# A diffusion block's front: first rows and gate weights loaded amid the input, sums that begin at the bias, more work on ACT, the weight transform ahead of its use

## The chip, the core and the metric

The kernel runs on one core of one Trainium2 chip. TensorE (PE) multiplies, VectorE (DVE), ScalarE (ACT) and GpSimd (POOL) work element by element, SyncE (SP) issues most DMAs. The metric is the device time of one execution in microseconds; the median of several runs counts.

## The reference

One layer: a normalised and modulated input goes through one projection into a Fourier group and a windowed attention group, both gated, and through one output projection. `x` is 1024 x 1024, `ctx` 256 x 1024, all fp32.

```python
def _ada(cond, w_ada, b_ada):
    mod = jax.nn.silu(cond) @ w_ada + b_ada
    return jnp.split(mod, 3, axis=-1)

sh_x, sc_x, g_x = [t[:, None, :] for t in _ada(c, w_ada[l], b_ada[l])]
sh_c, sc_c, g_c = _ada(c_ctx, w_ada[l], b_ada[l])
xn = _rms_norm(x, norm_g[l]) * (1.0 + sc_x) + sh_x
cn = _rms_norm(ctx, norm_g[l]) * (1.0 + sc_c) + sh_c
fx_in, fx_gate, qx, kx, vx, nx_gate = _split_proj(xn @ w_in[l])
fc_in, fc_gate, qc, kc, vc, nc_gate = _split_proj(cn @ w_in[l])
...
f_out = _fourier(fx_in, w_four[l]) * jax.nn.silu(fx_gate)
na_out = _neighbourhood_attention(qx, kx, vx, kc, vc, rel_bias[l]) * jax.nn.silu(nx_gate)
x_new = x + g_x * (jnp.concatenate([f_out, na_out], axis=-1) @ w_out[l])
```

`_fourier` is the real part of a 2-D DFT over positions and the 128 channels of each of 4 groups, then `@ w_four`.

## The kernel before

Every fp32 operand of a matmul is split into a rounded high part and the low rest (names ending in `h` and `l`: `xnh`, `xnl`, `wh`, `wl`), and a product is three matmuls: high by high, high by low, low by high. ACT mostly makes the high part (a cast or copy), DVE or POOL the low one (a subtraction).

The program runs in stages.

- *Input and turning.* `load_x` loads 8 tiles of `x` (128 rows each), `normalise` squares and sums them (ACT `Square`, or a DVE dot of `x` with itself), takes the root on POOL and scales the tile; `turn_x` transposes it on TensorE, and the results are copied to `xrt` (8 column blocks of 128, over all rows). `cond_row` broadcasts the 1 x 1024 row `c` over the partitions by a K=1 matmul, with the silu on ACT, into `sbc`.
- *ada dots.* For each of the 8 column blocks `i`, `load_wd` loads two 128 x 1024 tiles of the transposed `w_ada` (shift and scale), and `ada` issues a DVE dot of each with `sbc` (for `x`) and with `scc` (for the context), and behind each pair the three column operations of `ada_out`. A 256 KB gate weight comes with each block (`load_gate`, its cast and subtraction in `cut`).
- *Gate products* (L365). `modulate(i)` makes `xnh` (ACT), the modulated `xrt` (ACT or DVE) and `xnl` (DVE) in two halves of the rows, and 24 matmuls per block add to 8 PSUM banks.
- *Folds.* The DFT over positions is folded: `fold_zero`, `fold_ends`, `fold_middle` add and subtract rows of `xrt` (DVE); `fold_weights` transforms the Fourier columns of the weight by matmuls (`pw`, L469) and splits the result (`wab_h`, `wab_l`); `fold_products` multiplies (`pe`, `po`, `p`). `fourier_gate` takes silu of the gate products on ACT (L462).
- `turn_columns` finishes the transform over columns (`pp`, `pq`), with `w4h`/`w4l`, the transformed `w_four` (made from `wf` tiles by an add and a subtract on POOL, L595 and L597), ready for `ga` and `gb`.
- *Projections* of q, k, v and gates, the context's keys and values (`context_input`, `context_block`), and from some 160 us on the attention of 8 heads, interleaved with the rest of the projections and `gate_dot`, and last the output product.

The order on each engine is written by a planner that runs when the program is built: `chain` gives a list of steps with an engine and an assumed time, `when` and `at` hold a step until marks are set or a time is reached, and `issue` picks, whenever an engine is free by the planner's clock, the ready step with the lowest rank. Where a step may run on either of two engines (a list in the `chain`), whichever is free first takes it. The assumed times and ranks (`TC`, `RX`, `RG`, `RM`, `XS`, ... at the top) thus decide the order; on the chip each engine then runs its instructions in that fixed order and waits on semaphores. `XS` says how many tiles of `x` are loaded ahead of the first weights. SP issues loads in program order.

Of the kernel before, what the change touches and what calls it, by code (L numbers as in the profile page):

```python
# [11 lines left out]
F32 = mybir.dt.float32  # L12
# [7 lines left out]
P = 128  # L20
DM = 1024
KT = 8
TC, RX, RG, RM = 3.0, 2, 0, 2
TW, RT0, RT1, RT2, RH, D0, D1, NC = 4, 0, 4, -1, 1, 0, 0, 0
N0 = (3, 3, 2, 2)
XS = (8,)
LAG, PW, EB = 1, 8, 2
NP, NM, TL, WL = (0, 0, 0, 1, 0, 0, 0, 1), (6,) * 8, 0, 3
P0 = 1
# [15 lines left out]
def tile_hybrid_block(  # L45
# [47 lines left out]
    pool.memset(mhalf, -0.5)  # L93
    gsc = const.tile([P, 1], F32, name="gsc")
# [187 lines left out]
    def far_dot(wd, s, col, key, rank):  # L282

        chain((DVE_, 1.14, lambda: dot(wd, s, junk, col)), mark(*key), rank=rank)

    def ada(i, s, dsh, dav, name, rank):
        cols = wa.tile([P, 2], F32, name=f"cols{name}{i}")
        for j in range(2):
            when(((name, "s"), ("wd", i, j) if name == "x" else ("x", i, j)), lambda j=j: far_dot(wds[i, j], s, cols[:, j:j + 1], (name, i, j), rank))
        when(((name, i, 0), (name, i, 1), "vec"), lambda: chain((DVE_, 0.27, lambda: ada_out(i, cols, dsh, dav)), mark(name, i), rank=rank))  # L290

    def cond_row():

        for hf in range(2):
            hs = slice(hf * 512, hf * 512 + 512)
            pt = bank("pc", hf)
            mm(pt, ones1, sbc[0:1, hs], start=True, stop=True)
            chain((ACT_, 0.48, lambda hs=hs, pt=pt: act.activation(sbc[:, hs], pt, AF.Silu)), mark("x", "s") if hf else (lambda: None), rank=0)
# [14 lines left out]
    def load_gate(i):  # L313
# [3 lines left out]
        def cut():  # L317
            gate_w[i] = wh, wl = halves()
            chain(copy_by(512, WHO["gc"], wh, wr), mark("wh", i),
                  (DVE_, 0.6, lambda: dve.tensor_tensor(out=wl, in0=wr, in1=f(wh), op=ALU.subtract)),  # L320
# [3 lines left out]
    def turn_x(t):  # L324
        for hf in range(2):
            pt = bank("pt", hf if t < 4 else 1)
            for i in range(4):
# [4 lines left out]
                [(DVE_, 0.6, lambda: dve.tensor_copy(o, v)), (ACT_, 0.48, lambda: act.copy(o, v))],  # L332
                mark("turned", t, hf), rank=RT0 * t + (RT1 if hf else 0) + (RT2 if t > 3 else 0)))

    def normalise(t):
        x = xs[t]
        ss = wa.tile([P, 2], F32, tag="ss", bufs=8, name="ss")
        rs = wa.tile([P, 1], F32, tag="rs", bufs=8, name="rs")
        chain([(ACT_, 1.04, lambda: act.activation(sqx, x, AF.Square, accum_out=ss[:, 0:1])), (DVE_, 1.14, lambda: dot(x, x, junk, ss[:, 0:1]))],
              (DVE_, 0.07, lambda: dve.tensor_scalar(out=ss[:, 1:2], in0=ss[:, 0:1], scalar1=1.0 / DM, scalar2=EPS, op0=ALU.mult, op1=ALU.add)),  # L340
              (POOL_, 0.46, lambda: pool.tensor_tensor(out=rs, in0=ss[:, 1:2], in1=mhalf[:, 0:1], op=ALU.pow)),
              (DVE_, 0.67, lambda: dve.tensor_scalar_mul(x, x, rs)),
              (PE_, 1.7 if t < TW else 0.9, lambda: turn_x(t)), rank=RT0 * t + (RT2 if t > 3 else 0))

    def modulate(i):
# [6 lines left out]
        for hf in range(2):  # L352
# [1402 lines left out]
```

## Time and profile before

| | |
|---|---|
| runs | 605.64 us median of 3 (604.29 to 609.53) |
| profiled execution | 601.05 us, of which its span 599.3 |
| mean granted clock of TensorE | 0.98 |
| busy, share of the span | PE 91%, DVE 79%, ACT 59%, POOL 37% |
| instructions | PE 2923, DVE 967, ACT 742, POOL 196 |
| HBM read, written | 59.35 MB, 8.91 MB |

Times are microseconds from the start of the span. An operation is named by its line, engine, and the tiles it writes and reads (`out<-in`). "Idle before" is how long the engine stood still ahead of an instruction, with the instruction that released it. The busy share is an average over stages with different limits, so the rows below go by stretch. The clock column is the granted clock of TensorE, 1.00 being 2.4 GHz and 0.5 being 1.2 GHz.

### The profile page before, as it was taken

How to read it: one execution, taken by the hardware profiler on the slowest of the kernel's cores; microseconds unless marked ns; L12 is line 12 of the kernel's file. 1: busy time of each engine (PE TensorE's matmuls, PEld its weight loads, DVE VectorE, ACT ScalarE, POOL GpSimd, SP SyncE). 2: the span in 40 equal slices, each digit the busy share in tenths (PEclk: the TensorE clock that was granted, in tenths of full speed). 3: DMA queues.
4: the chain of work that ended last, by engine and by line, in shares of the span. 5: the costliest groups of instructions: out<-in, count | busy, mean ns of one | idle time of the engine just before them, and what ended most of it. 6: DMA issues, size and time to landing. Idle time of an engine off the chain costs nothing. (4 is left out here: it accounts for less than half of the span.)

```text
span 599.3 us, 8648 instructions
## 1 busy us (share of the span) xinstructions
PE 545.4 (91%) x2923; PEld 477.6 (80%) x2923; DVE 471.6 (79%) x967; ACT 353.4 (59%) x742; POOL 222.1 (37%) x196
## 2 busy tenths in 40 slices
PE   6699648899899999979999999999999798999997
PEld 4578538889677988979889889799898586787886
DVE  4999999985899678687895878977779959778342
ACT  6676035364634577767877878868767747654100
POOL 3100004014744635452545533444444937424300
PEclk9999968999999999999999999999999799999999
DMA  8970424025694242112032030321104563213152
GB/s 337 406 281 2 164 82 141 1 84 171 200 306 155 101 123 59 39 33 79 22 102 85 22 89 1 111 66 41 61 2 148 177 224 118 66 55 120 38 194 88
DMA packets 42889, 68.83 MB, mean 115 GB/s; under 512 B 3542, under 2 KB 25430, under 8 KB 42844
## 3 DMA queue, kind: packets, MB, share of 16 engines
q1 hardware_dynamic: 41836, 64.60, 32.1%
q0 software_dynamic: 1008, 3.67, 1.8%
q8 instruction: 23, 0.38, 0.3%
q14 instruction: 22, 0.18, 0.1%
HBM read 59.35 MB, written 8.91 MB: 114 GB/s over the span
## 5 line engine op out<-in xcount | busy, mean ns | idle before, releaser
L797 PE MATMUL pqkv<-wh,xnh 128*128 128x384 f32 x256 | 86.8, 339 | 0.0
L797 PE MATMUL pqkv<-wl,xnh 128*128 128x384 f32 x256 | 86.7, 339 | 0.0
L797 PE MATMUL pqkv<-wh,xnl 128*128 128x384 f32 x256 | 86.1, 336 | 0.0
L1174 ACT ACTIVATE pr<-pr,tr 128x640 f32<-128x640 f32 (+1 forms) x64 | 51.2, 801 | 28.4 <-DVE tr L1170 28.1
L1170 DVE CUSTOM_DVE_ANT_0 pr<-s,bias 128x640 f32<-128x640 f32 (+1 forms) x64 | 50.4, 788 | 21.9 <-PE s L1165 14.5
L703 POOL TENSOR_TENSOR hrs<-hss,mhalf 128x4 f32<-128x4 f32 (+1 forms) x34 | 37.7, 1113 | 60.7 <-DVE hss L700 53.1
L202 DVE TENSOR_TENSOR el<-e,eh 128x384 fp32r<-128x384 f32 (+2 forms) x71 | 50.7, 720 | 11.0 <-ACT eh L207 9.9
L207 ACT CAST eh<-e 128x384 fp32r<-128x384 f32 (+2 forms) x96 | 49.5, 528 | 1.4
L797 PEld LDWEIGHTS pqkv<-wl,xnh 128*128 128x128 f32 x256 | 48.1, 188 | 1.3
L797 PEld LDWEIGHTS pqkv<-wh,xnh 128*128 128x128 f32 x256 | 48.1, 188 | 1.3
L1266 ACT ACTIVATE e<-e 128x384 f32<-128x384 f32 (+1 forms) x64 | 31.5, 496 | 29.1 <-DVE e L1256 28.6
L797 PEld LDWEIGHTS pqkv<-wh,xnl 128*128 128x128 f32 x256 | 48.1, 188 | 0.7
L202 POOL TENSOR_TENSOR el<-e,eh 128x512 fp32r<-128x512 f32 x25 | 32.6, 1306 | 41.1 <-ACT eh L207 41.0
L202 POOL TENSOR_TENSOR wl<-wr,wh 128x384 fp32r<-128x384 f32 (+1 forms) x24 | 30.3, 1265 | 46.4 <-ACT wh L207 28.2
L1256 DVE TENSOR_TENSOR e<-st,biast 128x256 f32<-128x256 f32 (+2 forms) x80 | 34.0, 445 | 7.6 <-PE st L1248 6.8
L1163 PE MATMUL s<-ks,qs 128*128 128x256 f32 (+1 forms) x128 | 30.4, 318 | 9.1 <-DVE tr L1170 8.3
L1163 PEld LDWEIGHTS s<-ks,qs 128*128 128x128 f32 x128 | 23.1, 192 | 16.9 <-DVE tr L1170 13.2
L1247 PE MATMUL st<-qs,ks 128*128 128x512 f32 (+2 forms) x96 | 33.7, 353 | 0.3
L365 PE MATMUL pg<-xnh,w 128*128 128x512 f32 x128 | 31.3, 397 | 2.6 <-ACT xnh L356 2.6
L1248 PE MATMUL st<-qs,ks 128*128 128x512 f32 (+2 forms) x96 | 33.3, 347 | 0.0
L1443 PE MATMUL po<-oh,mh 128*128 128x512 f32 x88 | 32.3, 404 | 0.3 <-DVE gate L825 0.3
L365 PEld LDWEIGHTS pg<-xnh,w 128*128 128x128 f32 x128 | 23.9, 188 | 8.9 <-ACT xnh L356 3.3
(290 smaller groups left out, 1596.8 us busy)
## 6 DMA issues: line engine op xcount, KB each, us to landing
wd<-in_w_ada_t_dram SPq DMA_DIRECT2D x16, 512.0 KB, 8.9
wr<-in_w_in_dram SPq DMA_DIRECT2D x40, 192.0 KB, 2.7
wr<-in_w_in_dram SPq DMA_DIRECT2D x24, 256.0 KB, 4.1
x<-in_xb_dram SPq DMA_DIRECT2D x8, 512.0 KB, 6.4
wdg<-in_w_ada_t_dram SPq DMA_DIRECT2D x8, 512.0 KB, 5.3
owr<-in_w_out_dram SPq DMA_DIRECT2D x16, 256.0 KB, 2.9
y<-in_xb_dram SPq DMA_DIRECT2D x8, 512.0 KB, 6.6
out_dram<-y SPq DMA_DIRECT2D x15, 256.0 KB, 2.1
```

The lines of the kernel that those rows point to most:

```text
L202: return [(e, time(n), lambda eng=eng: eng.tensor_tensor(out=out, in0=in0, in1=in1, op=op)) for e, eng, time in (both[k] for k in who)]
L207: return [(e, time(n), lambda cp=cp: cp(out, in_)) for e, cp, time in (both[k] for k in who)]
L365: mm(pg[j][hf], gate_w[i][w][:, j * P:(j + 1) * P], x[i][:, hs], start=(i == 0 and g == 0), stop=(i == KT - 1 and g == 2))
L703: lambda: pool.tensor_tensor(out=rs[:, 0:nh], in0=ss[:, 0:nh], in1=mhalf[:, 0:nh], op=ALU.pow),
L797: mm(o, x[k][:, ts_], w, start=(k == 0 and n == 0), stop=(k == KT - 1 and n == 2))
L1163: mm(o, qs1[h][:, ts_], ks1[h][:, kk], start=st, stop=sp)
L1170: dve.tensor_tensor_reduce(out=pr, in0=sv, in1=bt, scale=-1.0, scalar=3.0e38, op0=ALU.add, op1=ALU.min, accum_out=tr[:, t:t + 1])
L1174: (ACT_, a_t(nl + CTX) + 0.15, lambda: act.activation(pr, pr, AF.Exp, bias=tr[:, t:t + 1], scale=-1.0, accum_out=sm[:, t:t + 1])),
L1247: mm(s, ks1[h][:, kk], qs1[h][:, qq], start=True, stop=False)
L1248: mm(s, ks2[h][:, kk], qs2[h][:, qq], start=False, stop=True)
L1256: dve.tensor_tensor(out=ew[:, u:v], in0=s3[:, u:v], in1=mixes[p, h][0][:, blocks], op=ALU.add)
L1443: mm(o, mf[k][m][:, ts_], wf[hf][k][w_], start=(k == 0 and n == 0), stop=(k == 3 and n == 2))
```

## The change

- Tiles 0 to 3 of `x` are loaded, then the shift and scale weights and the gate weight of block 0, then tiles 4 to 7 (`XS` is `(4, 8)`). The context's row `c_ctx` is loaded as one row beside `c` and broadcast by `cond_row` on TensorE, in place of a broadcast DMA of 512 KB.
- A dot starts from its bias column (and takes the norm's gain as its scale), so `ada_out` is gone; `vec_in` forms the combined bias once. The normalisation's epsilon is added by an ACT step behind `Square`, or is the start of the dot, in place of a DVE step. `gate_dot` starts from its bias too.
- The scaling of `x` and the copies from PSUM may go to ACT or DVE; the context's modulation is done by two ACT activations in place of a DVE step and an ACT copy. Assumed times of steps are changed.
- The fold stage issues the four gates first, then the eight `fold_weights`, with `fold_zero` and `fold_ends` after the fourth.
- The add and subtract on `wf` move from POOL in the fold stage to DVE in `turn_columns`, behind the splits of `pe` and `po`, and the `w4h`, `w4l` split with them.
- The planner also runs `issue` again for POOL and DVE when they become free after the set-up of the heads.

```diff
-TC, RX, RG, RM = 3.0, 2, 0, 2
...
-XS = (8,)
-LAG, PW, EB = 1, 8, 2
...
+TC, RX, RG, RM = 2.0, 2, 0, 2
...
+XS = (4, 8)
+LAG, EB, TL = 1, 2, 0
+NW = (0, 0, 0, 0, 1, 1, 1, 1)
...
-    def ada_out(i, cols, dsh, dav):
-        k = slice(i, i + 1)
-        dve.tensor_tensor(out=dsh[:, k], in0=cols[:, 0:1], in1=vec[:, V_BSH + i:V_BSH + i + 1], op=ALU.add)
-        dve.tensor_scalar(out=cols[:, 1:2], in0=cols[:, 1:2], scalar1=vec[:, V_BSC + i:V_BSC + i + 1], scalar2=1.0, op0=ALU.add, op1=ALU.add)
-        dve.tensor_tensor(out=dav[:, k], in0=cols[:, 1:2], in1=vec[:, V_NG + i:V_NG + i + 1], op=ALU.mult)
...
+    def dot(wd, s, jk, col, scale=1.0, first=0.0):
+        dve.tensor_tensor_reduce(out=jk, in0=wd, in1=s, scale=scale, scalar=first, op0=ALU.mult, op1=ALU.add, accum_out=col)
...
+    def squares(jk, x, ss):
+
+        act.activation(jk, x, AF.Square, scale=DM ** -0.5, accum_out=ss)
+        act.activation(ss, ss, AF.Identity, bias=epsc)
...
+    def vec_in():
+
+        dve.scalar_tensor_tensor(out=vec[:, V_BSC:V_BSC + KT], in0=vec[:, V_BSC:V_BSC + KT], scalar=1.0, in1=vec[:, V_NG:V_NG + KT], op0=ALU.add, op1=ALU.mult)
...
+        def column(j):
+            if j:
+                dot(wds[i, j], s, junk, dav[:, k], vec[:, V_NG + i:V_NG + i + 1], vec[:, V_BSC + i:V_BSC + i + 1])
+            else:
+                dot(wds[i, j], s, junk, dsh[:, k], 1.0, vec[:, V_BSH + i:V_BSH + i + 1])
...
-        chain([(ACT_, 1.04, lambda: act.activation(sqx, x, AF.Square, accum_out=ss[:, 0:1])), (DVE_, 1.14, lambda: dot(x, x, junk, ss[:, 0:1]))],
-              (DVE_, 0.07, lambda: dve.tensor_scalar(out=ss[:, 1:2], in0=ss[:, 0:1], scalar1=1.0 / DM, scalar2=EPS, op0=ALU.mult, op1=ALU.add)),
-              (POOL_, 0.46, lambda: pool.tensor_tensor(out=rs, in0=ss[:, 1:2], in1=mhalf[:, 0:1], op=ALU.pow)),
-              (DVE_, 0.67, lambda: dve.tensor_scalar_mul(x, x, rs)),
+        chain([(ACT_, 1.44, lambda: squares(sqx, x, ss)), (DVE_, 1.24, lambda: dot(x, x, junk, ss, 1.0 / DM, EPS))],
+              (POOL_, 0.46, lambda: root(rs, ss)),
+              [(ACT_, 1.06, lambda: act.mul(x, x, rs)), (DVE_, 0.75, lambda: dve.tensor_scalar_mul(x, x, rs))],
...
-                [(DVE_, 0.41, lambda: dve.tensor_scalar(out=v, in0=v, scalar1=av[:, k], scalar2=sh[:, k], op0=ALU.mult, op1=ALU.add)),
-                 (ACT_, 0.71, lambda: act.activation(v, v, AF.Identity, scale=av[:, k], bias=sh[:, k]))],
...
+                [(ACT_, 0.81, lambda: act.activation(v, v, AF.Identity, scale=av[:, k], bias=sh[:, k])),
+                 (DVE_, 0.55, lambda: dve.tensor_scalar(out=v, in0=v, scalar1=av[:, k], scalar2=sh[:, k], op0=ALU.mult, op1=ALU.add))],
...
-                dma(scc, c_ctx.broadcast_to([P, DM]))
...
-        fold_zero()
-        for i in range(EB):
-            fold_ends(i)
-        mid = fold_middle()
         for j in range(4):
             fourier_gate(j)
-            for _ in range(N0[j]):
+        mid = fold_middle()
+        for n in range(8):
+            fold_weights(n // 4, n % 4)
+            if n == 3:
+                fold_nyquist(0)
+                fold_zero()
+                for i in range(EB):
+                    fold_ends(i)
+            for _ in range(NW[n]):
                 next(mid)
...
-            if i == WL:
-                pool.tensor_tensor(out=wfr[0], in0=wfr[0], in1=wfr[1], op=ALU.add)
-            if i == WL + 1:
-                pool.tensor_tensor(out=wfr[2], in0=wfr[2], in1=wfr[1], op=ALU.subtract)
...
+        dve.tensor_tensor(out=wfr[0], in0=wfr[0], in1=wfr[1], op=ALU.add)
+        act.copy(w4h[0], wfr[0])
+        dve.tensor_tensor(out=wfr[2], in0=wfr[2], in1=wfr[1], op=ALU.subtract)
+        act.copy(w4h[1], wfr[2])
+        for m in range(2):
+            dve.tensor_tensor(out=w4l[m], in0=wfr[2 * m], in1=f(w4h[m]), op=ALU.subtract)
...
+        for e in (POOL_, DVE_):
+            at(free[e], lambda e=e: issue(e))
...
-        chain((DVE_, 0.33, lambda: dve.tensor_scalar(out=crt[:, i], in0=crt[:, i], scalar1=avc[:, k], scalar2=shc[:, k], op0=ALU.mult, op1=ALU.add)),
-              (ACT_, a_t(256), lambda: act.copy(h, crt[:, i])),
+        chain((ACT_, 0.42, lambda: act.activation(h, crt[:, i], AF.Identity, scale=avc[:, k], bias=shc[:, k])),
+              (ACT_, 0.42, lambda: act.activation(crt[:, i], crt[:, i], AF.Identity, scale=avc[:, k], bias=shc[:, k])),
```

The changed times and the new lists give the engines another order. On ACT, in the gate stage, before (casts of a gate weight are `w_N<-wr_M`, weight 5 the first here and weight 6 the second; `xnh4` is the modulated block 4):

```order
L207 CAST w_509<-wr_400 128x512
L356 ACTIVATE xnh4_338<-xrt1_98,sh_77,av_78 128x16x4x8 x2
L358 ACTIVATE xrt1_98<-xrt1_98,sh_77,av_78 128x16x32 x2
L207 CAST w_547<-wr_417 128x512
L356 ACTIVATE xnh5_339<-xrt1_98,sh_77,av_78 128x16x4x8 x2
```

The same place on ACT now (lines are those of the changed kernel):

```order
L207 CAST w_483<-wr_380 128x512
L207 CAST w_516<-wr_407 128x512
L358 ACTIVATE xnh4_359<-xrt1_100,sh_79,av_80 128x16x4x8 x2
L359 ACTIVATE xrt1_100<-xrt1_100,sh_79,av_80 128x16x32
L358 ACTIVATE xnh5_360<-xrt1_100,sh_79,av_80 128x16x4x8 x2
```

Both casts now stand ahead of block 4, where before the cast of weight 6 stood behind it; the second modulation of one half has gone to DVE.

On ACT, at the end of the gate products, before (`ef` is a fold of the ends, `gate_f` a gate, `h4` the high part of a fold):

```order
L490 CAST x0h_82<-x0_748 128x8
L501 ACTIVATE ef_760<-xrt0_97 128x1
L501 ACTIVATE ef_764<-xrt0_97 128x1
L462 ACTIVATE gate_f_768<-pg00_294 128x512
L462 ACTIVATE gate_f_768<-pg01_353 128x512
L523 CAST h4_771<-s2_773 128x512
```

And now:

```order
L359 ACTIVATE xrt1_100<-xrt1_100,sh_79,av_80 128x16x32
L463 ACTIVATE gate_f_697<-pg00_296 128x512
L463 ACTIVATE gate_f_697<-pg01_374 128x512
L463 ACTIVATE gate_f_700<-pg10_297 128x512
L463 ACTIVATE gate_f_700<-pg11_375 128x512
```

The gates now follow the last modulation at once, and the fold of the ends comes after them.

On DVE, in `turn_columns`, now (before, the two `w4l` rows stood ahead of `al`, and the two `wf` rows were POOL's):

```order
L114 TENSOR_TENSOR bl_1151<-po1_795,bh_1150 128x512
L624 TENSOR_TENSOR wf_671<-wf_671,wf_673 128x1024
L626 TENSOR_TENSOR wf_675<-wf_675,wf_673 128x1024
L629 TENSOR_TENSOR w4l0_1136<-wf_671,w4h0_1134 128x1024
L629 TENSOR_TENSOR w4l1_1137<-wf_675,w4h1_1135 128x1024
L631 CAST w64_1138<-w64_1138 4x512
L632 TENSOR_TENSOR w64_1138<-wfn_693,w64_1138 4x512
```

Four 128 x 1024 operations now stand between `bl` and `w64`.

## Rows read from the trace of the kernel before

**Rows 1.** Busy time by stretch: length; PE, PEld, DVE, ACT, POOL busy (instructions); clock; DMA share; GB/s.

```profile
0.00:24.00 24.00, 13.84 (x68) 9.57 (x68) 15.06 (x34) 16.43 (x30) 7.66 (x16) 1.00 0.94 363
24.00:70.00 46.00, 45.15 (x192) 35.92 (x192) 44.80 (x103) 24.38 (x36) 0.00 (x0) 1.00 0.45 169
70.00:83.00 13.00, 2.58 (x12) 2.50 (x12) 12.69 (x35) 1.27 (x4) 0.00 (x0) 0.64 0.38 128
...
101.00:124.00 23.00, 21.38 (x158) 20.07 (x158) 22.47 (x48) 9.15 (x18) 1.28 (x4) 0.93 0.01 2
...
136.00:160.00 24.00, 21.98 (x140) 20.20 (x140) 16.55 (x32) 13.31 (x30) 15.46 (x12) 1.00 0.65 209
160.00:548.00 388.00, 369.39 (x1971) 328.41 (x1970) 312.36 (x646) 268.79 (x582) 183.22 (x154) 0.99 0.29 92
```

**Rows 2.** What TensorE waited for, whole program: us in total, times, longest.

```profile
PE pw L469 <- ACT gate_f L462: 13.7, 2, 10.4
PE s L1163 <- DVE tr L1170: 8.3, 8, 3.5
```

**Rows 3.** What ACT waited for, 60 to 100 us, same columns.

```profile
ACT ef L501 <- DVE colsc L255: 17.2, 1, 17.2
```

**Rows 4.** Timeline of DVE: start, us, operation, out<-in, form; gate stage.

```profile
28.74 0.68 DVE L320 TENSOR_TENSOR w<-wr,w 128x512 fp32r<-128x512 f32 x1
29.34 0.15 DVE L250 TENSOR_TENSOR sh<-colsx,vec 128x1 f32<-128x1 f32 x1
...
29.73 1.22 DVE L255 CUSTOM_DVE_ANT_0 junk<-wd,sbc 128x1024 f32<-128x1024 f32 x1
30.87 0.09 DVE L255 DVE_READ_ACCUMULATOR2_ANT colsx<- 128x1 f32 x1
30.87 0.55 DVE L357 TENSOR_SCALAR xrt<-xrt,av,sh 128x512 f32<-128x512 f32 x1
```

**Rows 5.** Timeline of POOL, 95 to 100.2 us.

```profile
95.46 2.42 POOL L595 TENSOR_TENSOR wf<-wf 128x1024 f32<-128x1024 f32 x1
97.84 2.34 POOL L597 TENSOR_TENSOR wf<-wf 128x1024 f32<-128x1024 f32 x1
```

**Rows 6.** Timeline of DVE, the fold stage.

```profile
82.80 0.69 DVE L499 TENSOR_TENSOR ef<-xrt 128x512 f32<-128x512 f32 x1
...
86.90 0.69 DVE L526 TENSOR_TENSOR l<-s,h 128x512 fp32r<-128x512 f32 x1
...
97.13 3.60 DVE L526 TENSOR_TENSOR l<-s,h 128x512 fp32r<-128x512 f32 x1
```

**Rows 7.** Timeline of TensorE in the front; in brackets, idle before and releaser.

```profile
24.07 1.20 PE L365 MATMUL pg<-xnh,w 128*128 128x512 f32 x4 [1.82 <-ACT xnh L356]
...
80.50 3.67 PE L469 MATMUL pw<-cst,wtr 128*128 128x128 f32 x16 [10.42 <-ACT gate_f L462]
87.41 7.20 PE L469 MATMUL pw<-cst,wtr 128*128 128x128 f32 x48 [3.25 <-ACT gate_f L462]
...
100.79 0.45 PE L546 MATMUL pe<-wab_h,l 128*128 128x260 f32 x1 [2.54 <-DVE l L526]
```

**Rows 8.** Busy time by stretch, columns as in rows 1, at low clock.

```profile
100.90:104.50 3.60, 3.60 (x17) 3.52 (x18) 3.56 (x8) 1.07 (x2) 0.00 (x0) 0.53 0.03 7
472.90:479.90 7.00, 6.15 (x17) 4.97 (x18) 6.62 (x13) 3.39 (x6) 5.36 (x3) 0.51 0.55 172
```

**Rows 9.** Timeline of DVE, turn_columns.

```profile
123.71 2.36 DVE L632 TENSOR_TENSOR w4l<-wf,w4h 128x1024 fp32r<-128x1024 f32 x2 [0.27 <-ACT w4h L629]
...
133.43 0.42 DVE L114 TENSOR_TENSOR pl<-pp,ph 128x256 fp32r<-128x256 f32 x1 [0.49 <-ACT ph L113]
135.08 0.69 DVE L114 TENSOR_TENSOR ql<-pq,qh 128x512 fp32r<-128x512 f32 x1 [1.23 <-ACT qh L113]
```

**Rows 10.** Timeline of ACT, gate layers 3 to 5.

```profile
43.83 1.52 ACT L356 ACTIVATE xnh<-xrt,sh,av 128x512 fp32r<-128x512 f32 x2 [1.07 <-DVE av L252]
...
47.74 0.62 ACT L207 CAST w<-wr 128x512 fp32r<-128x512 f32 x1 [0.97 <-PE pg L365]
```

More of the change, by code (lines that the diff above doesn't have):

```diff
@@ L93, in tile_hybrid_block @@
     pool.memset(mhalf, -0.5)
+    epsc = const.tile([P, 1], F32, name="epsc")
+    pool.memset(epsc, EPS)
     gsc = const.tile([P, 1], F32, name="gsc")
@@ L296, in cond_row @@
             pt = bank("pc", hf)
-            mm(pt, ones1, sbc[0:1, hs], start=True, stop=True)
-            chain((ACT_, 0.48, lambda hs=hs, pt=pt: act.activation(sbc[:, hs], pt, AF.Silu)), mark("x", "s") if hf else (lambda: None), rank=0)
+            mm(pt, ones1, s[0:1, hs], start=True, stop=True)
+            chain((ACT_, 0.6, lambda hs=hs, pt=pt: act.activation(s[:, hs], pt, AF.Silu)), mark(name, "s") if hf else (lambda: None), rank=rank)
     def load_wd(i):
@@ L319, in cut @@
             chain(copy_by(512, WHO["gc"], wh, wr), mark("wh", i),
-                  (DVE_, 0.6, lambda: dve.tensor_tensor(out=wl, in0=wr, in1=f(wh), op=ALU.subtract)),
+                  (DVE_, 0.69, lambda: dve.tensor_tensor(out=wl, in0=wr, in1=f(wh), op=ALU.subtract)),
                   mark("wl", i), rank=RG + 10 * i)
@@ L386, in front @@
                 dma(sbc[0:1], c)
-                arrive(clock(), 0.1, lambda: at(TC, lambda: on([(PE_, 1.75, cond_row)], None, 0)))
+                dma(scc[0:1], c_ctx)
+                arrive(clock(), 0.1, lambda: at(TC, lambda: on([(PE_, 2.3, lambda: cond_row(sbc, "x", 0))], None, 0)))
+                when((("turned", 1, 1),), lambda: on([(PE_, 1.75, lambda: cond_row(scc, "c", 50))], None, 0))
             if t == 1:
@@ L390, in front @@
                 dma(cst, cs)
-                arrive(clock(), 1.0, mark("vec"))
+                arrive(clock(), 1.0, lambda: chain((DVE_, 0.1, vec_in), mark("vec"), rank=0))
         when(tuple(("turned", 3, hf) for hf in range(2)), lambda: bank_open(0))
@@ L407, in gate @@
                 load_next(i + 1)
-            if i == NC:
-                dma(scc, c_ctx.broadcast_to([P, DM]))
-                arrive(clock(), 4.0, lambda: chain((ACT_, 1.04, lambda: act.activation(scc, scc, AF.Silu)), mark("c", "s"), rank=50))
         when((("wl", i - 4),) if i > 3 else (), gate)
@@ L628, in turn_columns @@
         pool.memset(f(p64), 0.0)
-        act.copy(w4h[0], wfr[0])
-        act.copy(w4h[1], wfr[2])
-        for m in range(2):
-            dve.tensor_tensor(out=w4l[m], in0=wfr[2 * m], in1=f(w4h[m]), op=ALU.subtract)
         for m in range(4):
@@ L1061, in gate_dot @@
         arrive(clock(), 4.0, lambda: when(("sbc",), lambda: chain(
-            (DVE_, 1.15, lambda: dot(wd, cond[0], cond[1], gcol[:, k], 0.5)),
-            (DVE_, 0.07, lambda: dve.tensor_tensor(out=gcol[:, k], in0=gcol[:, k], in1=vec[:, V_BG + i:V_BG + i + 1], op=ALU.add)),
+            (DVE_, 1.25, lambda: dot(wd, cond[0], cond[1], gcol[:, k], 0.5, vec[:, V_BG + i:V_BG + i + 1])),
             mark("gcol", i), rank=3)))
```

59 lines of the change are left out of this document (18 added, 41 removed).

## The prediction

> **What bounds the kernel now.** I read the table of busy times by stretch first, then what each engine waited for, then the timelines where a wait is long. From 160 to 548 us TensorE works 369.39 of 388 us, and over 136 to 548 it idles 20.6 us in all [rows 1]. The change hardly touches that work, and only its order. The front is another matter: in 24 to 70 DVE works 44.80 of 46, TensorE 45.15 of 46; in 70 to 83 DVE 12.69 of 13 while TensorE works 2.58; in 101 to 124 DVE 22.47 of 23 [rows 1]. So up to 124 us the front ends when DVE ends, and DVE work taken out there should arrive. TensorE's largest waits say the same: 13.7 us for the gate activation L462 [rows 2], and further on 2.54 us for a DVE subtraction, L526 [rows 7]. The first of these was itself late because the ACT instruction ahead of it in program order, L501, had waited 17.20 us for the last context dots [rows 3].
>
> **The parts of the change, each with its cost.** The profiled execution took 601.05 us: a span of 599.3 and 1.75 around it. The median of the runs is 605.64, 4.6 above that. I work out a difference from the profile and set it off against the median.
>
> 1. *Sums that begin at the bias.* Every pair of ada dots is followed by three operations on one column (L250, L251, L252). One such trio holds DVE from 29.34 to 29.73, that is 0.39 us [rows 4]. There are 16 trios, and one of them ends before 24 us, where DVE is not full (15.06 of 24 busy [rows 1]). The other 15 are worth 15 x 0.39 = **5.85 us**. That a dot starting from a column takes no longer than 1.22 us is not shown in the trace: bounds 0 and 0.08 each (the accumulator read is a row of that size [rows 4]), so 0 to 2.6 us over 32 dots. I take 0, since the data streamed are the same. The 8 gate additions and the 10 normalisation steps on one column also go; DVE has room where they stand (16.55 of 24 in 136 to 160 [rows 1]), so 0.
>
> 2. *The weight transform off POOL.* POOL runs L595 and L597 from 95.46 to 100.18 [rows 5]. The DVE subtraction at 97.13 beside them took 3.60 us, against 0.69 for the same form at other places [rows 6]. DVE is the bound there, so **2.9 us** come back; and TensorE's 2.54 us wait, behind which its clock fell to 0.53 from 100.9 to 104.5 [rows 7, 8], goes with it. I don't count that twice, since TensorE follows DVE there. That it was POOL that slowed the subtraction is inferred from one coincidence, so the bounds are 0 and 2.9.
>
> 3. *What that costs later.* The add and the subtract become DVE work in `turn_columns`. Two 128x1024 operations there took 2.36 us [rows 9], so 2.36 more, but behind `al` and `bl`, which now come about as much earlier. What they delay is `p64` and `pl`, on which the Fourier columns wait. DVE has gaps of 0.49 and 1.23 us behind them [rows 9], both waits for ACT, which could take part of it. Bounds 0 and 2.4; I take **0.7 us lost**, nearer the gaps.
>
> 4. *More on ACT, less on DVE.* The planner now gives 8 of the second-half modulations to DVE instead of 5: 3 x 0.45 us (the row is 0.55 long, and I let it overlap the next by 0.1, as the 0.68 us row at 28.74 does [rows 4]) = **1.35 us lost** on DVE. Of the eight scalings of `x` four move to ACT, before 24 us.
>
> 5. *First rows and weights amid the input.* Rows 4 to 7 of `x` now stand behind two 512 KB and one 256 KB load. That is 1.3 MB, at the 363 GB/s of the first 24 us [rows 1] some 3.6 us later, and the ACT chain (squares, scalings, copies) then runs into the last transposes. By walking ACT's rows in the new order I get gate products from about 24.5 instead of 24.07 [rows 7] and DVE done with its share of the turning at 24.85, some 0.8 later than before: **0.8 us lost**; bounds 0 (the first weight is there earlier) and 3.6. The context row as 4 KB instead of a broadcast of 512 KB saves 1.4 us of queue, but the queue has slack behind it (DMA share 0.45 in 24 to 70 [rows 1]), so 0.
>
> 6. *A cast in front of a modulation.* In the order of before, ACT does `xnh4` (43.83) ahead of the cast of gate weight 6, and that cast is the one that waits for TensorE at 47.74 [rows 10]. In the new order the cast of weight 6 stands ahead of `xnh4`, and that of weight 3 ahead of `xnh1`; each needs the last product of the layer three before. So h4 can't begin before layer 3 is done: 24.5, four layers of 5.6 (45.15 of TensorE by 8 layers [rows 1]) and the first such wait of 1.45 give 48.35; plus 0.62 for the cast, plus 0.8 for the activation = 49.75. TensorE then idles some 1.4 us, twice, and the gate products end near 72.2 instead of 70.08 (80.50 less the 10.42 waited [rows 7]). That is covered, because of that very wait. DVE is not covered: from 24.4 us up to its first modulation of layer 4, which needs that activation, the new order gives it 10 dots (1.2 each start to start), 5 weight subtractions and 8 of `xnl` (0.6) and 4 modulations (0.5) [rows 4], 21.8 us together, so it is there at 46.2 and waits to 49.75: **3.5 us lost**. Bounds 0 (the queues stand a little differently) and 3.5.
>
> 7. *Gates first, then all folded weights, then the folds.* The gates no longer stand behind L501, so they run at once after the gate products, and the 64 transform matmuls (16 in 3.67 us, 48 in 7.20 [rows 7]) are done near 81. That removes TensorE's 10.42 us wait, but the casts of their results wait for the memory of the last context dot, at about 82.3 (the first fold row L499 began at 82.80 in before [rows 6]), and from there DVE has its folds as before. Worth 0 by itself: TensorE's idle time is not what ends last here.
>
> Sum: -5.85 - 2.9 + 0.7 + 1.35 + 0.8 + 3.5 = **-2.4 us**. The profile would read 598.6, the median 605.64 - 2.4 = **603.2**, 0.4% less.
>
> A rule that would speak against the change: the Trainium skill, TensorE: Matmul & The Clock Gate, section HAM oscillation, says that a TensorE left idle falls to half clock, and each new gap risks that. Here the clock stayed at 1.00 behind the 1.82 us wait at 24.07 and fell behind the 2.54 us one [rows 1, 7, 8], so two waits of 1.4 should leave it. By the rule each would cost some 1.6 us on TensorE (17 matmuls in 3.60 us [rows 8], 0.12 each at full clock), and the transform matmuls would end at 84 rather than 81, 1.7 past the last dot: the result 604.9 instead of 603.2.
>
> **The rivals.**
> - *All of DVE's saving arrives.* If the cast of item 6 doesn't hold h4 up, the 3.5 us stay saved, and 605.64 - 5.9 = 599.7; with the start of item 5 not late either, 598.9. For it: DVE waits in the gate stage hardly at all now, and my walk is by hand, with durations from one execution. Against it: the order is fixed by the program, and the cast waits 0.97 us already [rows 10].
> - *The new order lets attention run closer.* The planner's times change with all that is ahead of them, and with them the order of 1971 matmuls. There is 20.6 us of TensorE idle time in 136 to 548, 8.3 of it for the score transforms (`s` behind `tr`) [rows 1, 2]. A fifth of it, 4 us, added to the front gives 599.2; it can as well give nothing.
> - *It ends slower.* The same lottery the other way, as one mechanism: at 472.9 to 479.9 TensorE's clock is at 0.51 [rows 8], behind the longest wait for `tr`, 3.5 us [rows 2]. A second such collision costs that wait and half of 7 us, 7.0 in all: 603.2 + 7.0 = 610.2; two give 617.2. It decides against the change from 2.4 us on, and by more than 1% from 8.5 us on, so from the second on, or one with the front's gain gone as well.
> - *The gain is handed back.* If the two moved DVE operations come through whole (2.4 instead of 0.7) and POOL was not what stretched the subtraction, -2.4 becomes +2.2: 607.8, with the late start hidden again 607.0. Still no change.
>
> **How the numbers follow.** About 1% (6 us) is what a measurement of this kernel tells from no change: faster is below 599.6, slower above 611.7. My own case, 601 to 605, gets 0.36, the handed-back gain 0.14, both "same". All of DVE's saving, at the edge (599.7 and less): 0.20, of which 0.16 below. The closer attention 0.16, all below. Slower attention 0.14, of which 0.11 beyond 1%. With the remainders: faster 0.32, same 0.57, slower 0.11. The range goes from 597.5 (part of both fast cases stays below) to 609.0 (half of the slow one stays above); the likeliest case alone would be 601 to 605.
>
> **What would show each step.** Items 1 and 4: no L250 to L252 rows, and the last context dot at 82.3 (near 79 if item 6 fails). Item 6: a DVE wait of about 3 us near 46 to 50 for the activation of `xnh4`, and two TensorE waits of 1.4 us. Item 7: gates from 72 us, no 10 us wait on TensorE. Item 2: every L526 row at 0.69. Item 3: the add, the subtract and `w4l` between `bl` and `w64`, and shorter DVE gaps at `pl` and `ql` than 0.49 and 1.23 us. The rest of the program should then be shifted by 2 to 3 us with the same idle time; if TensorE's idle time from 136 us on differs by more than 3 us, the order of attention decided and not the front.

## The result and the profile after

The changed kernel takes 612.87 us (median of 4 runs, 611.4 to 614.32); the kernel before, timed beside it, 604.96. The ratio is 1.0141, with a 95% interval from 1.0094 to 1.0188: **slower by 1.4%**, where the prediction had 0.4% faster and a range that ends at 609. The profiled execution is 611.86 us with a span of 610.1, against 601.05 and 599.3: 10.8 us more. (The medians differ by 7.9: the profiled execution of before is 3.9 us below its median, that of the changed kernel 1.0.)

The busy time by stretch, columns as in [rows 1]:

```profile
0.00:24.00 24.00, 16.24 (x59) 11.48 (x60) 14.64 (x25) 17.88 (x31) 5.70 (x17) 0.93 0.91 342
24.00:70.00 46.00, 43.06 (x193) 34.55 (x192) 43.09 (x72) 22.81 (x32) 0.00 (x0) 1.00 0.40 155
70.00:83.00 13.00, 11.08 (x80) 10.05 (x78) 12.64 (x21) 4.14 (x8) 1.85 (x3) 1.00 0.54 178
...
101.00:124.00 23.00, 20.97 (x168) 19.61 (x167) 22.25 (x47) 7.86 (x16) 1.21 (x4) 1.00 0.00 1
...
136.00:160.00 24.00, 21.70 (x135) 20.02 (x136) 17.18 (x32) 12.58 (x30) 14.77 (x12) 1.00 0.63 204
160.00:548.00 388.00, 363.45 (x1931) 325.87 (x1930) 296.06 (x625) 269.69 (x580) 167.25 (x145) 0.98 0.27 88
548.00:610.10 62.10, 57.32 (x267) 47.41 (x265) 31.26 (x40) 10.75 (x16) 12.95 (x9) 1.00 0.34 119
```

The last stretch of the kernel before, which [rows 1] do not have:

```profile
548.00:599.30 51.30, 47.63 (x220) 39.27 (x218) 21.33 (x29) 3.11 (x5) 7.17 (x5) 1.00 0.31 108
```

From 136 us to the end TensorE is busy 21.70 + 363.45 + 57.32 = 442.5 of 474.1 us, so it idles 31.6. Before it was busy 439.0 there (21.98 and 369.39 [rows 1], and 47.63 from 548 on) of 463.3, and idled 24.3. So 7.3 us of the 10.8 are idle time and 3.5 the same matmuls at a lower clock (0.98 against 0.99 in the long stretch). DVE and POOL have less to do there than before (344.5 against 350.2 us, and 195.0 against 205.9). ACT has 7.8 us more (293.0 against 285.2); `n_oldctx` below shows that this is not the cause. The front, up to the first `ga` matmul, ends 1.0 us later than before:

```profile
136.72 0.39 PE L999 MATMUL ga<-ph,w4h 128*128 128x258 f32 x1 [1.59 <-DVE pl L114]
```

In the kernel before this row was:

```profile
135.70 0.28 PE L1007 MATMUL ga<-ph,w4h 128*128 128x258 f32 x1
```

Even this 1.0 us belongs to the two executions. Ten profiles, that of before and nine of the runs below, have the front of before, with TensorE's order the same up to `ga`, and their first `ga` stands between 135.61 and 138.81 us, in the middle at 136.7; with the changed front it is 136.72 here and 136.51 in `front_new`. So nearly all of the loss comes behind the part of the program on which the prediction worked longest. What TensorE waited for, over the whole program (columns as in [rows 2]):

```profile
PE pv L1270 <- DVE eh L1252: 6.8, 4, 3.1
PE s L1154 <- DVE tr L1161: 6.7, 7, 1.9
PE p L540 <- DVE x0h L492: 6.6, 1, 6.6
PE pe L545 <- ACT h L524: 4.5, 1, 4.5
...
PE s L1154 <- DVE ks L207: 3.5, 2, 2.0
PE ptq L863 <- DVE raw L694: 3.1, 3, 1.8
```

And three of the same in the kernel before:

```profile
PE pv L1279 <- DVE eh L1261: 5.4, 3, 3.1
...
PE s L1163 <- DVE ks L207: 0.6, 2, 0.3
PE ptq L873 <- DVE raw L704: 0.3, 1, 0.3
```

The 10.4 us wait for the gates [rows 2] is gone, and two waits of 6.6 and 4.5 in the fold stage stand in its place. In the attention stage the waits for `tr` are even a little shorter (6.7 against 8.3), but those for `ks` and `raw`, the preparation of the next head, have grown from 0.6 and 0.3 us to 3.5 and 3.1.

### The profile page after: what moved, and what is told of

Its sections match the earlier page's. It is cut to its first block, busy times and chain, and to the rows that moved or that the text cites. A ratio compares the mean times of both kernels' runs of the same rounds, so it can differ in the third digit from the quotient of the medians.

```text
span 610.1 us, 8603 instructions
## 1 busy us (share of the span) xinstructions
PE 550.3 (90%) x2927; PEld 483.3 (79%) x2927; DVE 464.1 (76%) x907; ACT 362.0 (59%) x752; POOL 204.6 (34%) x190
## 4 chain that ended last, share of the span: by engine, by line
PE 53%; DVE 26%; ACT 8%; issue 7%; DMA 4%; POOL 1%; SPq 0%; DVEq 0%; ACTq 0%; POOLq 0%
PE pqkv L787 14%; PE of L1613 7%; PE po L1434 5%; PE pv L1275 4%; PE pg L367 4%; PE st L1238 2%; PE s L1154 2%; PE st L1239 2%; DMA wr<-in_w_in_dram 2%; DVE junk L249 2%; PE s L1156 2%; DVE pr L1161 2%; DVE el L202 2%; DVE s L521 1%; PE png L809 1%
## 5 line engine op out<-in xcount | busy, mean ns | idle before, releaser
L202 POOL TENSOR_TENSOR el<-e,eh 128x512 fp32r<-128x512 f32 x24 | 31.2, 1301 | 53.5 <-ACT eh L207 49.8
L1257 ACT ACTIVATE e<-e 128x384 f32<-128x384 f32 (+1 forms) x64 | 31.6, 496 | 26.6 <-DVE e L1247 26.0
L202 POOL TENSOR_TENSOR wl<-wr,wh 128x384 fp32r<-128x384 f32 (+1 forms) x24 | 29.0, 1212 | 36.1 <-ACT wh L207 18.1
L1434 PE MATMUL po<-oh,mh 128*128 128x512 f32 x88 | 31.0, 393 | 0.9 <-DVE gate L815 0.9
```

What stands on the lines that cost most here:

```text
L202: return [(e, time(n), lambda eng=eng: eng.tensor_tensor(out=out, in0=in0, in1=in1, op=op)) for e, eng, time in (both[k] for k in who)]
L1434: mm(o, mf[k][m][:, ts_], wf[hf][k][w_], start=(k == 0 and n == 0), stop=(k == 3 and n == 2))
```

## The experiments

**First question: the front, or the order of the attention stage?** The planner's clock and its lists are cleared between the two, so the order behind the first `ga` depends on four small edits only: the context's normalisation, its modulation, the gate dots, and the extra call of `issue`. With these four undone TensorE's 2318 matmuls from the first `ga` on (the expectations count 2319) stand exactly as before; with these four alone they stand exactly as in the changed kernel.

`front_new` is the changed kernel without the four:

```diff
-        for e in (POOL_, DVE_):
-            at(free[e], lambda e=e: issue(e))
...
-        chain((ACT_, a_t(1024), n1), (POOL_, 0.46, n2), (DVE_, 0.67, n3), mark("xc", t))
+        chain((ACT_, a_t(1024), n1), (DVE_, 0.07, n2[0]), (POOL_, 0.46, n2[1]), (DVE_, 0.67, n3), mark("xc", t))
...
+        chain((DVE_, 0.33, lambda: dve.tensor_scalar(out=crt[:, i], in0=crt[:, i], scalar1=avc[:, k], scalar2=shc[:, k], op0=ALU.mult, op1=ALU.add)),
+              (ACT_, a_t(256), lambda: act.copy(h, crt[:, i])),
```

(and the gate dots' old form). `attn_new` is the kernel before with the reverse of this.

> The changed kernel with its attention stage as before: the four edits behind turn_columns (context normalisation, context modulation, gate dots, the planner's extra issue) undone, so that TensorE's 2319 matmuls from the first ga on stand in exactly the order of before. Theory A (the new order of the attention stage costs the time, the front is near even): the front arrives 1.0 us late as in the changed kernel, 605 to 607 us against 605. Theory B (the front's delay and its loads cost the time further on): near the changed kernel, 611 to 613.

Measured: 605.27 us, ratio to before 1.0013 (0.9983 to 1.0044).

> The kernel before with only those four edits of the attention stage, TensorE's order from the first ga on being exactly that of the changed kernel. Theory A: 611 to 615 us, TensorE idle some 7 us more from 136 us on and its clock low at about the same places as in the changed kernel. Theory B: 604 to 606.

Measured: 616.43 us, ratio 1.0177 (1.0108 to 1.0246). So the front is even, and **the new attention stage costs the whole of it**: theory A holds, B falls. That it is its order, and not the work that the four edits add, the second question shows. The two busy tables, of `front_new` first and of `attn_new` below, show it in the same way, TensorE idle 55.3 - 51.33 = 4.0 and 67.8 - 62.65 = 5.2 in the last stretch, and 19.7 and 24.6 of 388 in the long one:

```profile
160.00:548.00 388.00, 368.26 (x1960) 327.98 (x1959) 311.01 (x645) 266.99 (x579) 181.52 (x155) 0.99 0.29 93
548.00:603.30 55.30, 51.33 (x236) 42.30 (x235) 25.07 (x31) 5.51 (x9) 9.54 (x6) 0.99 0.29 100
```

```profile
160.00:548.00 388.00, 363.38 (x1908) 325.32 (x1908) 293.50 (x615) 266.63 (x575) 167.91 (x146) 0.97 0.28 88
548.00:615.80 67.80, 62.65 (x293) 51.81 (x291) 35.43 (x53) 14.29 (x23) 14.38 (x9) 1.00 0.31 109
```

Idle 4.9 us more in the long stretch, 52 fewer matmuls done in it, and the rest of them left for the end.

**Second question: which of the four edits?** One at a time on the kernel before, or one left out of the four.

> The kernel before with only the context normalisation's epsilon on ACT instead of DVE (two steps of 0.07 us leave DVE's chain, two of 0.3 us join ACT's). The work saved is under 0.2 us. Theory A says more precisely that any small edit gives the planner another order and so another time, either way: outside 604 to 606, by 2 us or more. If only the edits' work counts: 604.5 to 605.5.

Measured: 605.40 us, 1.0005 (0.9976 to 1.0034).

> The kernel before with only the context modulation as two ACT activations instead of a DVE step and an ACT copy (8 blocks). By work alone: 8 x 0.33 us leave DVE, about 8 x 0.4 join ACT, neither is the bound there: 604 to 606. By theory A another order and another time, 2 us or more away, either way.

Measured: 606.84 us, 1.0035 (1.0002 to 1.0069).

> The kernel before with only the planner's extra call of issue for POOL and DVE after the heads are set up. No instruction is added or taken away; TensorE's order agrees with that of before for the first 382 of the 2319 matmuls from ga on and then differs. If this edit carries the cost of the attention stage: 611 us or more. If the cost needs the edits together: 603 to 607.

Measured: 611.15 us, 1.0117 (1.0080 to 1.0154).

> The kernel before with only the gate dots beginning at their bias column (8 additions of one column gone). By work alone 8 x 0.07 us less on DVE: no change, 605. If this edit's new order carries the cost: 611 or more. The dots themselves will show whether a start from a column makes a dot longer: 1.28 us against 1.22 if so, 1.22 if the longer dots of the changed kernel come from elsewhere.

Measured: 605.13 us, 1.0003 (0.9982 to 1.0024).

> The kernel before with the new attention stage, but the context modulation as before: the four edits less one. If the order as such decides, this is a third order of the same work, anywhere from 603 to 616. If the context modulation on ACT is what costs (16 activations of 0.4 us on an engine that then comes late): back at 604 to 607.

Measured: 615.60 us, 1.0188 (1.0152 to 1.0223).

> The kernel before with the new attention stage, but the gate dots as before (from zero, with an addition). If the gate dots carry the cost: 604 to 607. If not: 610 to 617, as with all four edits.

Measured: 608.83 us, 1.0069 (1.0036 to 1.0103).

The extra call of `issue`, which adds and removes no instruction, costs 6 us by itself (7 by the ratio):

```diff
+        for e in (POOL_, DVE_):
+            at(free[e], lambda e=e: issue(e))
         done["open"] = 1
```

The other three, which are the second and third piece of the diff above the other way round and the gate dot's start at its bias, alone cost nothing or 2 us, although each gives another order too. So my wider claim, that any edit moves the time by 2 us or more, is wrong: `b_norm` and `b_gdot` have orders of their own and the time of before. `n_oldctx` says that the context's modulation on ACT is not the cause: without it ACT is busy 286.2 us from 136 us on (285.2 before), and the time is 615.60. `n_oldgdot` falls between its two expectations: the gate dots' edit costs nothing alone, but without it the other three cost 4 us and not 11. In `b_gdot` seven of the eight gate dots take 1.27 or 1.28 us, against 1.21 or 1.22 before, so a start from a column does make a dot longer.

Built for one engine at a time, the call for POOL leaves all of TensorE's order as before, the call for DVE gives the whole new order: it is DVE, told that it may take up its waiting steps behind the set-up of the heads, that starts the other sequence. With the order the planner also chooses some engines anew (four steps for `vs` go from POOL to DVE), but DVE's busy time from 136 us on stays, 349.2 us against 350.2; "order" below means both. (The changed kernel needs the call: without it its planner finds no next step.) In `b_issue` what TensorE waited for from 136 us on was:

```profile
PE s L1165 <- DVE tr L1172: 6.3, 11, 2.1
PE st L1249 <- DVE gate L1308: 4.1, 3, 1.7
PE s L1165 <- DVE ks L207: 3.5, 3, 2.6
```

The second and the third are waits that the kernel before has at under 0.3 and at 0.6 us. DVE is the engine that TensorE waits for, but not for one reason. Ahead of the 1.7 us wait for `gate` DVE itself waited for ACT; ahead of the 2.6 us wait for `ks` a DVE cast of `qs` took 2.57 us beside a POOL operation, where the cast of `ks`, of the same size and right behind it, took 0.42:

```profile
356.83 0.68 DVE L1292 TENSOR_TENSOR ot<-pv,ot 64x512 f32<-64x512 f32 x1 [1.77 <-ACT ot L1291]
358.48 1.35 DVE L202 TENSOR_TENSOR el<-e,eh 128x512 fp32r<-128x512 f32 x1 [0.97 <-ACT eh L207]
...
471.02 2.36 POOL L202 TENSOR_TENSOR ml<-omr,mh 128x1024 fp32r<-128x1024 f32 x1 [1.89 <-ACT mh L207]
471.08 2.57 DVE L207 CAST qs<-qs 64x512 fp32r<-64x512 f32 x1
```

Does the call make every order worse, or is each order a draw?

> The kernel before with only the planner's assumed DVE time for setting up the heads at 1.0 instead of 2.0 us: no instruction added, no extra issue, but DVE takes up its waiting steps earlier in the plan, and TensorE's order leaves that of before after 382 of 2319 matmuls, as it does with the extra issue. If any order in which DVE starts there earlier is worse: 609 to 616. If it is a matter of the single order: anywhere, and as likely 603 to 607.

Measured: 608.40 us, 1.0053 (1.0016 to 1.0089); nine of its ten executions lie between 602.88 and 611.77.

> The kernel before with the extra issue and an assumed DVE time of 3.5 instead of 2.0 us, so that DVE takes up its steps later in the plan; one more order. If the extra issue makes every order worse: 609 to 616. If the time is a matter of the single order: anywhere from 603 to 616.

Measured: 614.79 us, 1.0156 (1.0107 to 1.0205). Both are one number changed, the first without the call, the second in `b_issue`:

```diff
-OP, OD, OC = 4.5, 2.0, 8.0
+OP, OD, OC = 4.5, 1.0, 8.0
...
+OP, OD, OC = 4.5, 3.5, 8.0
```

The five orders with the call took 608.8 to 616.4 us, the four without it and with DVE's old time (that of before among them) 604.2 to 606.8, and `b_od0`, which lets DVE start earlier without the call, lies between. That speaks for DVE's earlier start as such being the worse sequence. `i_od`, in whose plan DVE starts later than in `b_issue` and which is no faster, speaks against it. Ten orders don't decide it, and why the orders with the call are the slow ones stays open.

**Third question: the front's terms.** These start from `front_new`, so that the old attention order carries the front's end through. They ran beside other executions of before than `front_new` did, so I compare ratios: a difference of two is uncertain by some 2.5 us.

`f_cast` holds the cast of gate weight `i` back until block `i-2` is modulated:

```diff
-        arrive(clock(), 2.0, lambda: when((("g", i - 3, 2, 1),) if i > 2 else (), cut))
+        arrive(clock(), 2.0, lambda: when((("g", i - 3, 2, 1), ("h", i - 2, 1), ("h", i - 2, 0)) if i > 2 else (), cut))
```

> front_new (the new front, the old attention order) with the cast of gate weight i held back until the modulation of block i-2 is issued, so that ACT does xnh4 and xnh1 ahead of the casts that wait for TensorE. If the cast in front of xnh4 costs what the trace of the changed kernel shows (DVE idle 2.69 us at 48.4) and DVE bounds the front: the DVE wait is gone, the last context dot ends 2.7 us earlier, 602.6 us. If something else then ends last (the transform weights' load, the casts): the wait is gone and the time stays at 605.

Measured: 603.18 us, ratio to before 0.9961 (0.9931 to 0.9991), so 3.1 us less than `front_new` by the ratios and 2.1 by the medians. DVE in the changed kernel, and then in `f_cast`, where block 4 begins:

```profile
48.32 0.08 DVE L249 DVE_READ_ACCUMULATOR2_ANT sh<- 128x1 f32 x1
51.09 0.55 DVE L360 TENSOR_SCALAR xrt<-xrt,av,sh 128x512 f32<-128x512 f32 x1 [2.69 <-ACT xnh L358]
```

```profile
45.15 1.28 DVE L362 TENSOR_TENSOR xnl<-xrt,xnh 128x512 fp32r<-128x512 f32 x2
46.35 0.54 DVE L361 TENSOR_SCALAR xrt<-xrt,av,sh 128x512 f32<-128x512 f32 x1
```

The wait at block 4 is gone (one of 0.84 us comes later), and the first `ga` stands at 134.98 instead of 136.51 in `front_new`. It is the only one of the fifteen versions run here whose interval lies below 1, by little, and the best of fifteen is in part picked by chance.

`f_wf` and `f_castwf` write the first `wf` operation ahead of the split into `al`, without and with the held cast.

```diff
+        dve.tensor_tensor(out=wfr[0], in0=wfr[0], in1=wfr[1], op=ALU.add)
         for m in range(4):
             split(pe_e[m][:, 0:260], ah[:, m], al[:, m])
...
-        dve.tensor_tensor(out=wfr[0], in0=wfr[0], in1=wfr[1], op=ALU.add)
```

> front_new with the first of the two wf operations on DVE put ahead of the split of pe into al, where DVE waited 1.10 us for ACT. It fills that wait: pl and the first ga come some 1.1 us earlier, 604.2 us. If what follows turn_columns is not sensitive to ga's start: 605.3 as front_new.

Measured: 607.90 us, 1.0044 (1.0018 to 1.0069).

> front_new with both of these. If the two add up and the front's end carries through to the end of the program: 605.3 - 2.7 - 1.1 = 601.5 us, faster than the kernel before. If the front's end does not carry through: 605.

Measured: 605.37 us, 1.0011 (0.9979 to 1.0042). Both miss, and for a reason that tells something: with nothing ahead of it to hold it in `turn_columns`, the program's builder put the operation far ahead, before the folds, where it waits for its load:

```profile
93.03 1.22 DVE L618 TENSOR_TENSOR wf<-wf 128x1024 f32<-128x1024 f32 x1 [4.38 <-DMA wf<-in_w_four_b_dram]
```

So they don't test what they were made for. But 4.38 + 1.22 us put on DVE in the fold stage moved the first `ga` from 136.51 to 140.62, and the time by 1.9 us (2.6 by the medians): DVE bounds the front, as the prediction had it.

`f_pool` puts both `wf` operations back on POOL:

```diff
+            if i == 3:
+                pool.tensor_tensor(out=wfr[0], in0=wfr[0], in1=wfr[1], op=ALU.add)
+            if i == 4:
+                pool.tensor_tensor(out=wfr[2], in0=wfr[2], in1=wfr[1], op=ALU.subtract)
...
-        dve.tensor_tensor(out=wfr[0], in0=wfr[0], in1=wfr[1], op=ALU.add)
...
-        dve.tensor_tensor(out=wfr[2], in0=wfr[2], in1=wfr[1], op=ALU.subtract)
```

> front_new with the two wf operations back on POOL in the fold stage, as in the kernel before, and nothing else changed. If POOL's 128x1024 operations stretch a DVE operation beside them: a DVE row of about 3.6 us (0.7 alone) between 86 and 100 us again, worth +2.9, against 2.4 saved in turn_columns: about 605.8 us. If the 3.60 us row of the kernel before was something else: no such row, and 603 us.

Measured: 605.70 us, 1.0029 (1.0000 to 1.0058). DVE beside POOL's two operations:

```profile
92.30 2.68 POOL L590 TENSOR_TENSOR wf<-wf 128x1024 f32<-128x1024 f32 x1 [7.66 <-DMA wf<-in_w_four_b_dram]
94.94 2.52 POOL L592 TENSOR_TENSOR wf<-wf 128x1024 f32<-128x1024 f32 x1
...
93.29 1.97 DVE L522 TENSOR_TENSOR s<-ef 128x256 f32<-128x256 f32 x1
95.18 0.68 DVE L114 TENSOR_TENSOR wab_l<-pw,wab_h 128x512 fp32r<-128x512 f32 x1
95.78 1.96 DVE L522 TENSOR_TENSOR s<-ef 128x256 f32<-128x256 f32 x1
```

Two rows of a form that takes 0.42 us elsewhere (at 92.46 in the changed kernel) take 1.97 and 1.96, together 3.1 us too long; the one between them, which reads PSUM, has its 0.68. Each of the two ends 0.28 us behind the end of the POOL operation beside it. So POOL does stretch DVE's operations. All ten profiles with the front of before have the long `l` row, of 3.60 to 4.80 us; none of the six with `wf` on DVE has one. What the move is worth in all is less clear: `f_pool` takes 3.1 us longer than `front_new` from the last dot to the last fold and 1.75 less from there to `ga`, and its time is 1.0 us more by the ratios, which is inside the noise. The Trainium skill, GPSIMD Engine Reference, section Key points, states that GpSimd shares its SBUF interfaces with VectorE, in contention with operations of two SBUF inputs; these rows agree.

`f_trio` makes the ada dots start from zero again, with the three column operations behind each pair (`vec_in` left out):

```diff
+            dot(wds[i, j], s, junk, cols[:, j:j + 1])
...
+            dve.tensor_tensor(out=dsh[:, k], in0=cols[:, 0:1], in1=vec[:, V_BSH + i:V_BSH + i + 1], op=ALU.add)
+            dve.tensor_scalar(out=cols[:, 1:2], in0=cols[:, 1:2], scalar1=vec[:, V_BSC + i:V_BSC + i + 1], scalar2=1.0, op0=ALU.add, op1=ALU.add)
+            dve.tensor_tensor(out=dav[:, k], in0=cols[:, 1:2], in1=vec[:, V_NG + i:V_NG + i + 1], op=ALU.mult)
```

> front_new with the 16 pairs of ada dots as before: from zero, with the three column operations of the kernel before behind each pair. In the changed kernel a dot that starts from a column takes 1.28 us, one that takes its scale from a column too 1.34, and a pair 2.72; before a dot took 1.22 and a pair with its trio some 2.8. If the dots' starts are what makes them longer: dots at 1.22 again and the last context dot about 1.4 us later, 606 to 607 us. If the longer dots have another cause, they stay at 1.28 and 1.34 with the trios on top: 5 us later, 610.

Measured: 607.21 us, 1.0046 (1.0020 to 1.0073), some 2 us over `front_new`. That is not the price of the trios: in this order DVE's wait of item 6 shrank to three of 0.65 us and less, and the first `ga` stands at 136.83, only 0.3 us behind `front_new`. The rows of the dots do answer the question. In it a dot and its read are, first row and second, as before; below them the two kinds of dot of the changed kernel:

```profile
74.43 1.23 DVE L249 CUSTOM_DVE_ANT_0 junk<-wd,scc 128x1024 f32<-128x1024 f32 x1
75.58 0.08 DVE L249 DVE_READ_ACCUMULATOR2_ANT colsc<- 128x1 f32 x1
```

```profile
69.25 1.28 DVE L249 CUSTOM_DVE_ANT_0 junk<-wd,scc,vec 128x1024 f32<-128x1024 f32 x1
70.46 0.08 DVE L249 DVE_READ_ACCUMULATOR2_ANT shc<- 128x1 f32 x1
70.58 1.34 DVE L249 CUSTOM_DVE_ANT_0 junk<-wd,scc,vec 128x1024 f32<-128x1024 f32 x1
71.85 0.08 DVE L249 DVE_READ_ACCUMULATOR2_ANT avc<- 128x1 f32 x1
71.96 1.28 DVE L249 CUSTOM_DVE_ANT_0 junk<-wd,scc,vec 128x1024 f32<-128x1024 f32 x1
```

A pair now takes 71.96 - 69.25 = 2.71 us. In `f_trio` a pair with its trio takes 75.97 - 73.17 = 2.80. A start from a column adds 0.06 us to a dot, and a scale from a column 0.06 more. For dots in a row, as the context's are, the saving is 0.09 us a pair, not 0.39.

## Why the prediction was wrong, point by point

- **The step that failed** is the sentence "The change hardly touches that work, and only its order", and with it the zero that the sum carries for everything behind `turn_columns`. The order was worth +9.8 us of the 10.8 between the two profiles, and 7.7 by the ratios (1.0141 against 1.0013 of `front_new`). It stood among the rivals ("It ends slower") with 0.14. That the price which this rival puts on one event, 7 us, is near the loss is luck: its mechanism, a second collision like the one before 473 us, was only partly right. What came was not one long wait with a clock drop but several of 1.5 to 3 us, some close together:

```profile
385.67 0.35 PE L1154 MATMUL s<-ks,qs 128*128 128x256 f32 x1 [2.00 <-DVE ks L207]
387.99 0.90 PE L1154 MATMUL s<-ks,qs 128*128 128x384 f32 x2 [1.73 <-DVE tr L1161]
...
439.04 0.55 PE L1270 MATMUL pv<-eh,vs 128*128 128x256 f32 x1 [3.06 <-DVE eh L1252]
```

  In stretches of 20 us the clock is under 1 in five between 300 and 480 us (these four and, at 0.97, that from 420, whose drop goes on behind 440); in the kernel before in one, 460 to 480 [rows 8]:

```profile
300.00:320.00 20.00, 17.20 (x84) 14.88 (x83) 16.67 (x31) 15.59 (x36) 9.08 (x11) 0.91 0.29 90
...
380.00:400.00 20.00, 16.27 (x80) 13.97 (x78) 16.75 (x33) 14.46 (x32) 7.65 (x10) 0.91 0.20 63
...
440.00:460.00 20.00, 19.91 (x106) 18.75 (x105) 13.72 (x32) 13.85 (x30) 5.64 (x5) 0.94 0.12 37
460.00:480.00 20.00, 17.91 (x100) 15.83 (x99) 16.92 (x32) 16.78 (x32) 10.29 (x10) 0.91 0.36 125
```

- **Item 1, the second failure**: the dots. I priced the removed trios at 5.85 us and the new dots' starts at 0, and kept 2.6 as the bound. By the rows the starts cost 0.18 us a pair, 2.7 in all. Another 0.12 stands between a read and the next dot, as it did before between two dots, and without the trios that happens 16 times and not 11, 0.6 us. What is left of 5.85 is 2.5 us: 0.09 for a pair of dots in a row, 0.2 where another operation follows each dot. The last context dot ended at 85.51 (82.3 forecast), behind which the folds start:

```profile
85.43 0.08 DVE L249 DVE_READ_ACCUMULATOR2_ANT avc<- 128x1 f32 x1
86.21 1.29 DVE L114 TENSOR_TENSOR wab_l<-pw,wab_h 128x512 fp32r<-128x512 f32 x2 [0.70 <-ACT wab_h L113]
```

  I chose the zero end of a bound because "the data streamed are the same"; but a dot with column operands is another form of instruction, and no row of before had it.

- **Item 2** was right: the fold stage lost its stretched operation. From the last context dot to the last fold DVE took 85.51 to 123.51, 38.0 us, against 40.6 before (82.80 [rows 6] to 123.44), and `f_pool` brings the stretching back. **Item 3**, 0.7 us lost, measured 1.0: TensorE waits 1.59 us for `pl` at the first `ga`.

- **Item 5** was too small. DVE was to be done with the turning at 24.85; it was at 26.13, where before its first modulation stood at 24.05. That is 2.1 us lost, not 0.8:

```profile
26.13 0.68 DVE L361 TENSOR_TENSOR xnl<-xrt,xnh 128x512 fp32r<-128x512 f32 x1
```

  **Item 4** came as forecast, eight modulations on DVE instead of five.

- **Item 6** was right in place and mechanism, and a little large: DVE waited 2.69 us from 48.4 on, not 3.5 from 46.2, because the late start and the longer dots brought it there later. ACT shows the cast waiting for TensorE and `xnh` of block 4 behind it:

```profile
49.72 0.62 ACT L207 CAST w<-wr 128x512 fp32r<-128x512 f32 x1 [4.98 <-PE pg L367]
50.25 1.51 ACT L358 ACTIVATE xnh<-xrt,sh,av 128x512 fp32r<-128x512 f32 x2
```

  `f_cast` shows that the cast in front is the cause; that its removal reaches the end of the program is just clear of the noise.

- **Item 7** was right: the gates ran at 72 to 76.5 us, the 10 us wait went, and it was worth nothing. TensorE waited 6.6 and 4.5 us for the folds instead, and did the first of their products at half clock until 101 us.

- **The clock in the gate stage**, whose fall was weighed against the change, stayed at 1.00 in 24 to 70 us with two waits there of 1.52 and 1.42 us, as the rows of before had it. In the attention stage the drops come behind waits, but a wait's length does not settle it: the 3.10 us wait for `eh` at 266.33 in the profile of before left the clock at 1.00, and the same wait, 3.06 us at 268.04, in that of `front_new` brought 266 to 276 us down to 0.83.

By these two profiles the front's sum was -2.4 us and is +1.0. Up to the last context dot it was to gain 0.2 and lost 2.7: the dots save 3.3 less and item 5 costs 1.3 more, while item 6 costs 1.4 less than forecast (2.69, and a wait of 0.56 that DVE had before is gone) and 0.3 us of small operations now stands behind it. The fold stage then saves 2.6 instead of 2.9, and item 3 costs 1.0 instead of 0.7. Items 4 and 5 have no run of their own, `f_wf` missed item 3, and this split is read from one execution each. `front_new` confirms that this front is no change by its time. The rest is the order.

## What to carry to other kernels

Where a planner writes the order, ask of every edit whether the planner's state carries over, and count an edit that only moves a decision (here one call that adds no instruction) among those with the largest possible effect: the work that it adds (here none) puts no bound on what it can cost. Split the program where the planner starts anew, and run the two halves apart: two runs settled here what no reading of the rows could. And an instruction form that the trace does not show, if it occurs 32 times on the engine that bounds the stage, gets the middle of its bounds and not the end that fits the story.

## What the runs showed of the hardware

- A DVE dot over 128 x 1024 takes 1.22 us with constants, 1.28 with its start value from a column (`b_gdot` alone changes this: 1.27 to 1.28), 1.34 with its scale from a column too.
- Two DVE operations with two SBUF inputs beside a POOL operation on 128 x 1024 took 1.97 and 1.96 us instead of 0.42 (`f_pool`), and one with a single input 2.57 (`b_issue`); each ended 0.27 or 0.28 us behind the POOL operation. One that reads PSUM kept its 0.68. Before, one of 0.69 came to 3.60 beside two of them, ending 0.55 us behind the second.
- The same instruction order varies more than the difference of many edits: the kernel before from 600.88 to 608.51 us in the 25 executions beside `front_new`.
